# Two-chunk MLP: up-projection as seven half-size products, ScalarE's own GELU, second weight parts on VectorE

## The chip, the cores and the metric

The kernel runs on one core of a Trainium2 chip. The metric is the device time of one execution in microseconds (us): the median over the runs of a kernel. The engines are TensorE (PE, with its weight loads as PEld), VectorE (DVE), ScalarE (ACT), GpSimd (POOL) and SyncE (SP), which issues the DMA transfers. Each engine works through its own queue of instructions in order; a wait on another engine holds up all that stands behind it in the same queue.

## The reference

The reference is one layer of an encoder (width 1024), applied with the same weights to a sequence of 512 rows and to one of 1024. The layer has a mixer (windowed attention and gated linear attention, one input projection, one output projection) and then a gated MLP. The change lies in the MLP:

```python
h = rmsnorm(x, n_ffn_pre)
a, g = jnp.split(h @ w_up, 2, axis=-1)          # w_up: 1024 x 5632
a = dwconv_centred(a, conv_w, conv_b)           # width 3 along the rows of the sequence
f = (jax.nn.gelu(a, approximate=True) * g) @ w_down   # w_down: 2816 x 1024
return x + rmsnorm(f, n_ffn_post)
```

## The kernel before

**Chunks and stages.** Rows are worked in three chunks of 512: chunk 0 is the first sequence, chunks 1 and 2 are the second. The stages are: the input projection of chunk 0; that of chunks 1 and 2, woven with the mixer of the first sequence; the output projection of chunk 0; the MLP of chunk 0 (`m0`), woven with the mixer of the second sequence; the output projections of chunks 1 and 2; and last the MLP of chunks 1 and 2 together (L1240), which runs from about 1340 us to the end.

**Three matmuls for one.** Operands are kept as a first part (`hi`, rounded to 16 bits, or to fp32r) and a second part (`lo`, what is left). `mm3` (L348) forms hi x hi, hi x lo and lo x hi. Each matmul takes 128 rows of the inner dimension, 128 output columns (or rows) and 512 rows of a chunk.

**An MLP block.** The 2816 columns of the MLP are 22 blocks of 128. `Mlp.up(b)` (L1029) computes, for both chunks, the block's columns of `a` and then those of `g`: `gemm_fm` (L483) runs over the eight row tiles of `w_up` in two weight units of four tiles, and uses each unit for both chunks, 24 matmuls. So a block has four units and 96 matmuls. The results stay in PSUM and go through these steps, the same for each chunk: ScalarE copies `a` with the middle tap's weight and the bias (L1047); VectorE adds the outer two taps from PSUM and, at the seam of the chunks, one column (L1045); GELU is written out as a square on ScalarE (L1059), a product on VectorE (L1060), tanh on ScalarE (L1064) and a product on VectorE (L1065); VectorE multiplies with `g` from PSUM (L1079); ScalarE rounds to the first part of `f` (L1080), VectorE forms the second (L1083).

**The order.** `ORDER` (L298) runs blocks 0, 1, 2, 3, then the down-projection of group 0 (blocks 0 to 2), then 4, 5, 6, the down-projection of group 1, and so on; the last group has four blocks. A down-projection (`down`, L1095) has a unit for each block and half of the 1024 output columns, each used for the eight row tiles of the two chunks, 24 matmuls; its sums are added to `y` on VectorE (L1115). In the last one `Post` normalises the rows, adds the residual and stores them.

**The weights.** `_Weights` (L70) serves the units in a list written out beforehand (`units_ffn`, L322). At each `next()` it first runs what was set down for later (`later(n, fn)` runs `fn` at the n-th `next()` from then: the steps above hang on this), then forms the first part of the unit three ahead on ScalarE (`_hi`, L107), and the second part of the unit two ahead on VectorE (`_lo`, L113), and issues loads further ahead. A load (`_load`, L86) brings two units, 512 KB, into one of six `w_raw` tiles. First parts have four buffers, second parts three: the first part three units ahead goes into the buffer that the unit before the present one leaves. In the MLP of chunk 0 the weights are also measured, for the scale that takes them into 16 bits (`Group`, L237; `Rows` does the same for the activations).

**Memory around the change.** The tiles that the last stage takes on the right side of the SBUF (`f2`, `two`, L1239) lie where earlier stages had theirs. `load_mix` (L949) loads the mixer's result in eight tiles for each output projection. `attention` has small tiles `m` (8 buffers) and `den` (4).

## Time and profile before

| | |
|---|---|
| median of 3 runs | 2058.14 us (2057.96 to 2066.22) |
| the profiled execution | 2062.58 us |
| its span, first to last instruction | 2060.8 us |
| TensorE busy / granted clock, mean | 1897.4 us (92%) / 0.97 |
| VectorE, ScalarE, GpSimd busy | 1177.3, 968.7, 241.5 us |
| MLP of chunks 1 and 2 | from about 1340 us to the end |

How to read the profile's lines: a group has line, engine, operation, output <- inputs with their shapes, and a count; then busy time in us and the mean of one in ns; then the engine's idle time just before these instructions and what ended it. A line of the timeline has start, duration, engine, line, operation, and in brackets the idle time before it. L351, L352 and L353 are the three matmuls of `mm3`. The names of the activations of chunks 1 and 2 in the last stage are `d` and `c`; `w_hi` and `w_lo` are the parts of the weights, `bank` is a PSUM bank, `ya` the MLP's tile between the steps, `f` its result.

### The profile page before, as it was taken

How to read it: one execution, taken by the hardware profiler on the slowest of the kernel's cores; microseconds unless marked ns; L12 is line 12 of the kernel's file. 1: busy time of each engine (PE TensorE's matmuls, PEld its weight loads, DVE VectorE, ACT ScalarE, POOL GpSimd, SP SyncE). 2: the span in 40 equal slices, each digit the busy share in tenths (PEclk: the TensorE clock that was granted, in tenths of full speed). 3: DMA queues.
4: the chain of work that ended last, by engine and by line, in shares of the span. 5: the costliest groups of instructions: out<-in, count | busy, mean ns of one | idle time of the engine just before them, and what ended most of it. 6: DMA issues, size and time to landing. Idle time of an engine off the chain costs nothing. (4 is left out here: it accounts for less than half of the span.)

```text
span 2060.8 us, 31557 instructions
## 1 busy us (share of the span) xinstructions
PE 1897.4 (92%) x11912; PEld 1184.9 (57%) x11912; DVE 1177.3 (57%) x2363; ACT 968.7 (47%) x1858; POOL 241.5 (12%) x529
## 2 busy tenths in 40 slices
PE   4999899999988787988998999999999999999996
PEld 3486444887754544455565567745565646464655
DVE  4555673342548787886666545764355454545556
ACT  5665564232557776878345335534323232413232
POOL 3112110000222212120110202210000000000002
PEclk9999999999999999999998999999999999999998
DMA  6766984335559999974334268631121111111132
GB/s 199 223 180 164 208 182 138 114 94 196 195 156 167 206 203 183 186 172 143 99 97 135 88 212 285 223 111 44 52 62 41 52 52 52 41 57 57 52 132 83
DMA packets 389613, 274.74 MB, mean 133 GB/s; under 512 B 173874, under 2 KB 342066, under 8 KB 389460
## 3 DMA queue, kind: packets, MB, share of 16 engines
q1 hardware_dynamic: 389460, 272.72, 50.2%
q8 instruction: 94, 1.54, 0.3%
q14 instruction: 59, 0.48, 0.1%
HBM read 191.83 MB, written 47.28 MB: 116 GB/s over the span
## 5 line engine op out<-in xcount | busy, mean ns | idle before, releaser
L351 PE MATMUL bank<-c,w_hi 128*128 128x512 f16 (+1 forms) x816 | 312.4, 383 | 4.4 <-DVE y L1115 3.7
L353 PE MATMUL bank<-c,w_lo 128*128 128x512 f16 (+1 forms) x816 | 311.4, 382 | 4.4 <-DVE w_lo L120 4.4
L352 PE MATMUL bank<-c,w_hi 128*128 128x512 f16 (+1 forms) x816 | 311.4, 382 | 0.0
L353 PEld LDWEIGHTS <-w_lo 128*128 128x128 f16 x1360 | 135.0, 99 | 167.4 <-issue 9.1
L351 PEld LDWEIGHTS <-w_hi 128*128 128x128 f16 x1360 | 135.8, 100 | 158.8 <-issue 11.6
L111 ACT ACTIVATE w_hi<-w_raw,up_up 128x512 f16<-128x512 f32 x176 | 125.8, 719 | 214.5 <-PE bank L352 107.6
L352 PEld LDWEIGHTS <-w_hi 128*128 128x128 f16 x1360 | 135.0, 99 | 158.4 <-issue 14.1
L352 PE MATMUL bank<-w_lo,f 128*128 128x512 f32 x528 | 212.9, 403 | 5.0 <-DVE w_lo L118 5.0
L351 PE MATMUL bank<-w_hi,f 128*128 128x512 f32 x528 | 213.2, 411 | 2.8 <-DVE y L1115 1.8
L353 PE MATMUL bank<-w_hi,f 128*128 128x512 f32 x528 | 211.2, 400 | 0.0
L111 ACT ACTIVATE w_hi<-w_raw 128x512 fp32r<-128x512 f32 x144 | 90.3, 630 | 243.4 <-PE bank L353 191.3
L120 DVE SCALAR_TENSOR_TENSOR w_lo<-w_raw,up_up,w_hi 128x512 f16<-128x512 f32 x176 | 131.3, 748 | 107.4 <-PE bank L353 49.9
L118 DVE TENSOR_TENSOR w_lo<-w_raw,w_hi 128x512 fp32r<-128x512 f32 x144 | 98.5, 687 | 122.0 <-PE bank L352 96.4
L1045 DVE SCALAR_TENSOR_TENSOR ya<-bank,cvt,ya 128x511 f32<-128x511 f32 x176 | 108.0, 614 | 73.8 <-ACT ya L1047 67.5
L1115 DVE TENSOR_TENSOR y<-bank,y 128x512 f32<-128x512 f32 x144 | 96.3, 687 | 88.6 <-PE bank L353 88.4
L353 PE MATMUL bank<-d,w_lo 128*128 128x512 f16 x352 | 133.4, 379 | 0.9 <-DVE w_lo L120 0.9
L351 PE MATMUL bank<-d,w_hi 128*128 128x512 f16 x352 | 133.5, 379 | 0.1
L352 PE MATMUL bank<-d,w_hi 128*128 128x512 f16 x352 | 133.4, 379 | 0.0
L254 ACT ACTIVATE w_junk<-w_raw 128x512 bf16<-128x512 f32 (+1 forms) x136 | 85.3, 627 | 98.5 <-DMA w_raw<-in_w_up_dram 50.0
L352 PEld LDWEIGHTS bank<-w_lo,f 128*128 128x128 f32 x528 | 100.9, 191 | 30.1 <-DVE w_lo L118 8.8
L632 DVE SCALAR_TENSOR_TENSOR p<-t,rs,p 128x512 f16<-128x512 f32 (+2 forms) x96 | 88.5, 925 | 51.2 <-ACT p L625 50.7
L351 PEld LDWEIGHTS bank<-w_hi,f 128*128 128x128 f32 x528 | 100.6, 191 | 29.1 <-ACT y L1113 1.7
(193 smaller groups left out, 3658.8 us busy)
## 6 DMA issues: line engine op xcount, KB each, us to landing
w_raw<-in_w_up_dram SPq DMA_DIRECT2D x88, 512.0 KB, 4.4
w_raw<-in_w_in_dram SPq DMA_DIRECT2D x44, 512.0 KB, 4.4
w_raw<-in_w_down_dram SPq DMA_DIRECT2D x36, 512.0 KB, 4.0
mix<-mx SPq DMA_DIRECT2D x24, 512.0 KB, 9.3
xin<-in_x_sample_dram SPq DMA_DIRECT2D x16, 512.0 KB
w_raw<-in_w_out_dram SPq DMA_DIRECT2D x32, 256.0 KB, 6.2
xin<-x SPq DMA_DIRECT2D x16, 512.0 KB, 4.6
bias<-in_nbias_dram SPq DMA_DIRECT2D x8, 832.0 KB
```

Source lines behind the costliest of these rows:

```text
L111: self.nc.scalar.activation(out=self.hi[i], in_=raw, func=ACTF.Copy, scale=1.0 if group is None else group.scale)
L118: self.nc.vector.tensor_tensor(out=lo, in0=raw, in1=hi.bitcast(F32), op=ALU.subtract)
L120: self.nc.vector.scalar_tensor_tensor(out=lo, in0=raw, scalar=group.scale, in1=hi, op0=ALU.mult, op1=ALU.subtract)
L254: nc.scalar.activation(out=junk[:, :raw.shape[1]], in_=raw, func=ACTF.Square, accum_out=self.sums[:, self.at:self.at + 1])
L351: nc.tensor.matmul(out, ah, bh, start=start, stop=False)
L352: nc.tensor.matmul(out, ah, bl, start=False, stop=False)
L353: nc.tensor.matmul(out, al, bh, start=False, stop=stop)
L632: nc.vector.scalar_tensor_tensor(out=p[:, n:2 * n], in0=t[:, kf:T], scalar=rs, in1=p[:, 0:n], op0=ALU.mult, op1=ALU.subtract)
L1045: nc.vector.scalar_tensor_tensor(out=out, in0=src, scalar=cw[:, j:j + 1], in1=out, op0=ALU.mult, op1=ALU.add)
L1115: nc.vector.tensor_tensor(out=y[t][:, cols], in0=ps[t], in1=y[t][:, cols], op=ALU.add)
```

## The change

In the MLP of chunks 1 and 2, blocks 3 to 21 (`PLAIN = 3`) no longer compute four products of weight halves and activations but seven (the Strassen-Winograd form of a 2 x 2 block product). The weights of a block are four quarters: `a11`, `a12` (upper and lower 512 rows of the columns for `a`), `a21`, `a22` (those for `g`); the activations are four: `b11`, `b21` (chunk 1), `b12`, `b22` (chunk 2). A product is 4 row tiles x 3 matmuls.

- **Weight sums.** A block has seven units. `_prep`, four units ahead, scales the two loaded tiles in place on ScalarE (two copies of 1024 columns) and forms four sums of 512 columns on GpSimd. First parts of all seven are formed on ScalarE as before, second parts of all seven on VectorE, without a scale.
- **Activation sums.** `sums` forms three new quarters `t1` to `t3` (in `quarters`), twelve steps woven with the first blocks, and puts the fourth in the place of `b12` after block 2, four steps issued at once. A step is a GpSimd sum, two VectorE sums, a ScalarE copy and a GpSimd difference.
- **Output sums.** `up7` copies two products out of PSUM on ScalarE, adds the other five on VectorE, each to what is in SBUF, and has two sums on GpSimd. Convolution and product then read from SBUF and not from PSUM.
- **GELU.** With two chunks (blocks 0 to 2 too), square, product, tanh and product become one ScalarE function, `Gelu_apprx_tanh`, and the product with `g` uses the scale without the factor 0.5. The MLP of chunk 0 keeps the old steps.
- **Everywhere.** Second parts are formed three units ahead (`LO` 3, before 2) with four buffers (before 3). Scales leave room for the sums (factor 4). `m` has 6 buffers, `den` 3. The first sequence's output projection holds seven of its eight `mix` tiles at a time (`held`). Gain rows and row tiles are placed in a pool `pre` that is given back before the last stage, which takes `f2`, `two`, `work` and `quarters`. In the last stage `f`'s two steps come at the third and fourth `next()` after a changed block's last product; before, at the second and third.

The core of the diff:

```diff
-    LOAD, SCALE, HI, LO = 1, 2, 3, 2
+    LOAD, SCALE, PREP, HI, LO = 1, 2, 4, 3, 3
...
+    def _prep(self, i):
+        if len(self.units[i]) == 7 or self.units[i][7]:
+            return
+        group, n = self.units[i][5], NK * 64
+        for t in self.block[i]:
+            self.nc.scalar.activation(out=t, in_=t, func=ACTF.Copy, scale=group.scale)
+        a11, a12, a21, a22 = (t[:, k * n:(k + 1) * n] for t in self.block.pop(i) for k in range(2))
...
+            self.nc.gpsimd.tensor_tensor(out=t, in0=x, in1=y, op=op)
...
+        s1 = total(a21, a22, ALU.add)
+        s2 = total(s1, a11, ALU.subtract)
+        s4 = total(a12, s2, ALU.subtract)
+        s3 = total(a11, a21, ALU.subtract)
+        for j, x in enumerate((a11, s1, s2, a12, s4, s3, a22)):
+            self.raw[i + j] = x
...
+        if len(self.units[i]) > 7:
+            self.nc.vector.tensor_tensor(out=lo, in0=raw, in1=hi, op=ALU.subtract)
...
+        self._upto("prep", self._prep, i + self.PREP)
         self._upto("hi", self._hi, i + self.HI)
         self._upto("lo", self._lo, i + self.LO)
...
+            if kind == "up" and n == 2 and i >= PLAIN:
+                for j in range(7):
+                    units.append((w_up, 0, 4, (i * 128, FF + i * 128), 128, G_UP[i], False, j))
...
+        def sums(self, b):
...
+            self.right = (b11, t1, t2, b21, b22, t3, b12)
+            todo = [(t1, b12, b11, ALU.subtract), (t3, b22, b12, ALU.subtract), (t2, t3, b11, ALU.add)]
+            for out, x, y, op in ([(b12, b21, t2, ALU.subtract)] if b else todo):
+                for k in range(n):
+                    hi, lo = (self.work.tile([128, CH], F32, name=nm, tag=nm) for nm in ("u", "v"))
+                    nc.gpsimd.tensor_tensor(out=hi, in0=x[0][:, k], in1=y[0][:, k], op=op)
+                    nc.vector.tensor_tensor(out=lo, in0=x[1][:, k], in1=y[1][:, k], op=op)
+                    nc.vector.tensor_tensor(out=hi, in0=hi, in1=lo, op=ALU.add)
+                    nc.scalar.activation(out=out[0][:, k], in_=hi, func=ACTF.Copy)
+                    nc.gpsimd.tensor_tensor(out=out[1][:, k], in0=hi, in1=out[0][:, k], op=ALU.subtract)
+                    yield 1
...
+            def product(j, pool, fn):
+                wh, wl = W.next()
+                xh, xl = self.right[j]
+                ps = bank(pool)
+                for k in range(NK // 2):
+                    mm3(ps, (wh[:, k, :], wl[:, k, :]), (xh[:, k], xl[:, k]), k == 0, k == NK // 2 - 1)
+                later(1, lambda: fn(ps))
...
+            def p6(ps):
+                add(u, ps, x)
+                nc.gpsimd.tensor_tensor(out=y, in0=u, in1=v, op=ALU.add)
+
+            def p7(ps):
+                add(u, ps, u)
+                nc.gpsimd.tensor_tensor(out=v, in0=u, in1=v, op=ALU.add)
+            product(0, dense, lambda ps: keep(x, ps))
+            yield 1
+            product(1, dense, lambda ps: keep(v, ps))
+            yield 1
+            product(2, spare_banks, p6)
+            yield 1
+            product(3, dense, lambda ps: add(x, ps, x))
+            yield 1
+            product(4, dense, lambda ps: add(y, ps, y))
+            self.act(b, two, [x, y], (2, 3))
+            yield 1
+            product(5, spare_banks, p7)
+            yield 1
+            product(6, spare_banks, lambda ps: add(u, ps, u))
+            self.gate(b, two, f, [u, v], (3, 4))
+            yield 1
...
+            def whole(i):
+                nc.scalar.activation(out=two[i][:, 1], in_=two[i][:, 0], func=ACTF.Gelu_apprx_tanh)
+            for at, fn in zip(steps, (conv, poly, gelu) if n == 1 else (conv, whole)):
...
+                else:
+                    yield from self.up(i)
+                    _run(self.sums(i))
...
-            box["mix"] = list(load_mix(0, box["mx"], 8))
+            box["mix"] = held(load_mix(0, box["mx"], 7), 7)
...
+    _weave(m12.run(ORDER), m12.sums(0), 20, 12)
```

More of the change, by code (lines that the diff above doesn't have):

```diff
@@ L87, in _load @@
         if i in self.raw:
+            return
+        if len(self.units[i]) > 7:
+            if self.units[i][7] == 0:
+                self.block[i] = [self._whole(i, c0) for c0 in self.units[i][3]]
             return
@@ L108, in _hi @@
         raw, group = self.raw[i], self.units[i][5]
+        whole = len(self.units[i]) > 7
         hi = self.pool.tile([128, self.width], F32R if group is None else FP16, name="w_hi", tag="w_hi", bufs=4)
         self.hi[i] = hi[:, :raw.shape[1]]
[L111 removed]
+        self.nc.scalar.activation(out=self.hi[i], in_=raw, func=ACTF.Copy,
+                                  scale=1.0 if group is None or whole else group.scale)
     def _lo(self, i):
         raw, hi, group = self.raw[i], self.hi.pop(i), self.units[i][5]
[L115 removed]
+        lo = self.pool.tile([128, self.width], F32R if group is None else FP16, name="w_lo", tag="w_lo", bufs=4)
         lo = lo[:, :raw.shape[1]]
[L117 removed]
+        if len(self.units[i]) > 7:
+            self.nc.vector.tensor_tensor(out=lo, in0=raw, in1=hi, op=ALU.subtract)
+        elif group is None:
             self.nc.vector.tensor_tensor(out=lo, in0=raw, in1=hi.bitcast(F32), op=ALU.subtract)
@@ L954, in load_mix, with held, rest @@
             yield t
+    def held(tiles, n):
+        ready = [next(tiles) for _ in range(n)]
+        def rest():
+            yield ready.pop(0)
+            while ready:
+                ready.extend(t for t in [next(tiles, None)] if t is not None)
+                yield ready.pop(0)
+        return rest()
     class Post:
@@ new lines, in up7, with add, keep @@
+        def up7(self, b):
+            f = [f(b) for _, _, f, _ in self.chunks]
+            self.f[b] = f
+            two = [pool.tile([128, 2, CH], F32, name="ya", tag="two") for pool in self.two]
+            u, v = (self.work.tile([128, CH], F32, name=nm, tag=nm) for nm in ("u", "v"))
+            x, y = (t[:, 1] for t in two)
+            def product(j, pool, fn):
[5 more added lines that the diff above has]
+                later(1, lambda: fn(ps))
+            def add(out, ps, x):
+                nc.vector.tensor_tensor(out=out, in0=ps, in1=x, op=ALU.add)
+            def keep(out, ps):
+                nc.scalar.activation(out=out, in_=ps, func=ACTF.Copy)
+            def p6(ps):
[20 more added lines that the diff above has]
+            yield 1
@@ L1039, in up, with act @@
             yield from gemm_fm([(c[1], pa) for c, pa in zip(self.chunks, pas)])
+            self.act(b, two, pas, (1, 2, 3))
+            yield n
+            pgs = [bank(self.banks[i]) for i in range(n)]
+            yield from gemm_fm([(c[1], pg) for c, pg in zip(self.chunks, pgs)])
+            self.gate(b, two, f, pgs, (2, 3))
+            yield n
+        def act(self, b, two, pas, steps):
+            cw, n = cvt[:, b, :], len(self.chunks)
             def conv(i):
@@ L1065, in gelu, with gate @@
                 nc.vector.scalar_tensor_tensor(out=s, in0=s, scalar=1.0, in1=ya, op0=ALU.add, op1=ALU.mult)
-            def each(steps, fn):
+            def whole(i):
+                nc.scalar.activation(out=two[i][:, 1], in_=two[i][:, 0], func=ACTF.Gelu_apprx_tanh)
+            for at, fn in zip(steps, (conv, poly, gelu) if n == 1 else (conv, whole)):
                 for i in range(n):
-                    later(steps, lambda i=i: fn(i))
-            each(1, conv)
-            each(2, poly)
-            each(3, gelu)
-            yield n
-            pgs = [bank(self.banks[i]) for i in range(n)]
-            yield from gemm_fm([(c[1], pg) for c, pg in zip(self.chunks, pgs)])
+                    later(at, lambda i=i, fn=fn: fn(i))
+        def gate(self, b, two, f, pgs, steps):
+            undo = G_UP[b].undo[:, 1:2] if len(self.chunks) == 1 else G_UP[b].undo[:, 0:1]
             def prod(i):
                 s, fh = two[i][:, 1], f[i][0]
-                nc.vector.scalar_tensor_tensor(out=s, in0=s, scalar=G_UP[b].undo[:, 1:2], in1=pgs[i], op0=ALU.mult, op1=ALU.mult)
+                nc.vector.scalar_tensor_tensor(out=s, in0=s, scalar=undo, in1=pgs[i], op0=ALU.mult, op1=ALU.mult)
                 nc.scalar.activation(out=fh, in_=s, func=ACTF.Copy)
@@ L1083, in rest @@
                 nc.vector.tensor_tensor(out=f[i][1], in0=two[i][:, 1], in1=f[i][0].bitcast(F32), op=ALU.subtract)
-            each(2, prod)
-            each(3, rest)
-            yield n
+            for at, fn in zip(steps, (prod, rest)):
+                for i in range(len(self.chunks)):
+                    later(at, lambda i=i, fn=fn: fn(i))
         def residual(self, i):
@@ L1136, in run @@
             for kind, i in order:
-                yield from (self.up(i) if kind == "up" else self.down(i))
+                if kind == "down":
+                    yield from self.down(i)
+                elif len(self.chunks) == 1 or i >= PLAIN:
+                    yield from (self.up if len(self.chunks) == 1 else self.up7)(i)
+                elif i < PLAIN - 1:
+                    yield from self.up(i)
+                else:
+                    yield from self.up(i)
+                    _run(self.sums(i))
     def after(n, gen):
```

63 lines of the change are left out of this document (41 added, 22 removed).

## The prediction

> **What bounds the kernel now.** I read the page's busy shares and slices first, then a table of busy time by stage, then the groups of instructions and the timeline inside the last stage, where the change lies.
>
> ```profile
> PE 1897.4 (92%) x11912; PEld 1184.9 (57%) x11912; DVE 1177.3 (57%) x2363; ACT 968.7 (47%) x1858; POOL 241.5 (12%) x529
> ```
>
> ```profile
> PE   4999899999988787988998999999999999999996
> ```
>
> ```profile
> 1331.00:1995.00 664.00, 659.95 (x2999) 371.77 (x2998) 348.24 (x539) 213.67 (x337) 7.11 (x14) 1.00 0.19 57
> 610.00:930.00 320.00, 273.60 (x1400) 154.17 (x1400) 258.85 (x620) 241.12 (x452) 71.80 (x182) 0.95 0.96 183
> ```
>
> The columns of the last fence are stretch, length, busy PE, PEld, DVE, ACT, POOL, granted clock, DMA share, GB/s. From 1331 to 1995 us, nearly the whole two-chunk MLP, TensorE has work for 659.95 of 664 us at a clock of 1.00, while VectorE is busy 348, ScalarE 214 and GpSimd 7 us. There the time is the number of matmuls times their spacing. Busy time per matmul overstates the spacing, since neighbours overlap, so I take it from starts:
>
> ```profile
> 1500.02 0.38 PE L351 MATMUL bank<-d,w_hi 128*128 128x512 f16 x1
> ...
> 1519.87 0.38 PE L353 MATMUL bank<-c,w_lo 128*128 128x512 f16 x1
> ...
> 1520.32 0.39 PE L352 MATMUL bank<-w_lo,f 128*128 128x512 f32 x1
> ...
> 1552.94 0.39 PE L352 MATMUL bank<-w_lo,f 128*128 128x512 f32 x1
> ```
>
> The first pair is 92 spacings apart: 19.85 / 92 = 0.2158 us for an up-projection matmul. The second is 141 apart: 32.62 / 141 = 0.2313 us for a down-projection one.
>
> ```profile
> L352 PE MATMUL bank<-d,w_hi 128*128 128x512 f16 x337 | 127.7, 379 | 0.0
> L352 PEld LDWEIGHTS <-w_hi 128*128 128x128 f16 x673 | 65.9, 98 | 78.6
> ```
>
> L352 has 673 weight loads here for the matmuls of both chunks (337 of `d` and 336 of `c`): each matmul already loads its own 128 columns. A product that serves one activation matrix therefore loses no shared load, and 0.2158 us holds for the new products.
>
> **TensorE: the gain.** An up block is 2 column blocks x 2 chunks x 8 row tiles x 3 = 96 matmuls; as seven products it is 7 x 4 x 3 = 84. Nineteen of 22 blocks change: 19 x 12 = 228 matmuls x 0.2158 = **49.2 us** less, if everything else stays hidden. A changed block has 18.1 us instead of 20.7, and one product 12 x 0.2158 = 2.59 us.
>
> **VectorE and ScalarE in a changed block.** Rows from 1360 to 1995 us (the wide ACT row and the table load from the whole run):
>
> ```profile
> L1045 DVE SCALAR_TENSOR_TENSOR ya<-bank,cvt,ya 128x511 f32<-128x511 f32 x84 | 62.9, 748 | 62.7 <-ACT ya L1047 62.0
> L120 DVE SCALAR_TENSOR_TENSOR w_lo<-w_raw,up_up,w_hi 128x512 f16<-128x512 f32 x82 | 61.2, 748 | 80.7 <-PE bank L353 41.8 <-issue 23.5 <-PE bank L352 14.5
> L1115 DVE TENSOR_TENSOR y<-bank,y 128x512 f32<-128x512 f32 x80 | 55.3, 691 | 84.2 <-PE bank L353 84.0
> L1079 DVE SCALAR_TENSOR_TENSOR ya<-ya,undo_up,bank 128x512 f32<-128x512 f32 x42 | 31.3, 744 | 17.4 <-PE bank L353 17.4
> L1065 DVE SCALAR_TENSOR_TENSOR ya<-ya 128x512 f32<-128x512 f32 x44 | 30.4, 692 | 2.4
> L1060 DVE SCALAR_TENSOR_TENSOR ya<-ya 128x512 f32<-128x512 f32 x43 | 29.5, 687 | 16.0 <-ACT ya L1059 16.0
> L1083 DVE TENSOR_TENSOR f<-ya,f 128x512 fp32r<-128x512 f32 x42 | 29.1, 692 | 28.5 <-ACT f L1080 28.5
> L118 DVE TENSOR_TENSOR w_lo<-w_raw,w_hi 128x512 fp32r<-128x512 f32 x38 | 26.1, 688 | 15.6 <-PE bank L352 12.3 <-PE bank L353 2.9
> L1045 DVE SCALAR_TENSOR_TENSOR ya<-bank,cvt,ya 128x1 f32<-128x1 f32 x42 | 9.1, 216 | 5.1 <-PE bank L353 5.1
> ```
>
> ```profile
> L111 ACT ACTIVATE w_hi<-w_raw,up_up 128x512 f16<-128x512 f32 x81 | 57.8, 722 | 159.9 <-PE bank L352 76.8 <-DVE y L1115 72.9 <-DVE ya L1045 9.6
> L1047 ACT ACTIVATE ya<-bank,cvt 128x512 f32<-128x512 f32 x42 | 32.3, 769 | 44.4 <-PE bank L353 44.4
> L1059 ACT ACTIVATE ya<-ya 128x512 f32<-128x512 f32 x43 | 26.8, 623 | 20.8 <-DVE ya L1045 20.8
> L1080 ACT ACTIVATE f<-ya 128x512 fp32r<-128x512 f32 x42 | 26.4, 630 | 67.5 <-DVE ya L1079 67.5
> L111 ACT ACTIVATE w_hi<-w_raw 128x512 fp32r<-128x512 f32 x39 | 24.6, 632 | 105.6 <-PE bank L353 66.1 <-PE bank L352 39.0
> L1113 ACT ACTIVATE y<-bank 128x512 f32<-128x512 f32 x16 | 9.6, 598 | 18.8 <-PE bank L353 18.2
> ```
>
> ```profile
> L376 ACT ACTIVATE junk<-xin 128x1024 bf16<-128x1024 f32 x24 | 25.1, 1047 | 12.2 <-DMA xin<-x 12.0
> ```
>
> ```profile
> 955.31 1.28 ACT L1064 ACT_TABLE_LOAD   x1
> ```
>
> VectorE, before: 4 second parts x 0.748, 4 taps x 0.748, 2 edges x 0.216, polynomial 2 x 0.687, GELU end 2 x 0.692, product 2 x 0.744, `rest` 2 x 0.692 = 12.0 us of 20.7. After: 7 second parts x 0.688 (4.8), 5 sums out of PSUM x 0.691 (3.5), taps and edges as before (3.4), product and `rest` (2.9): **14.6 us of 18.1**. ScalarE, before: 4 x 0.722 + 2 x (0.769 + 0.623 + 0.623 + 0.630) = 8.2. After: 2 scaled copies of 1024 columns at 1.047 plus 0.09 for the scale operand (0.722 - 0.632), 7 first parts x 0.632, 2 copies out of PSUM x 0.598, 2 x (0.769 + 0.623 + 0.630): **11.9 us of 18.1**. Both fit, and the down blocks between give slack. The built-in GELU was not run; I take the 0.623 us of the ScalarE functions in its place. Its table costs one load, 1.28 us in the last row; were tables loaded twice a block, ScalarE would have 14.5 of 18.1 us, still hidden.
>
> **GpSimd, and the price of sharing with VectorE.** GpSimd now adds 128x512 tiles: four for the weights and two for the outputs of each block.
>
> ```profile
> 562.04 4.25 POOL L476 TENSOR_TENSOR stg<-stg,gg 128x512 f32<-128x512 f32 x3 [3.31 <-DVE stg L475]
> 583.41 0.73 POOL L476 TENSOR_TENSOR stg<-stg,gg 128x256 f32<-128x256 f32 x1
> L476 POOL TENSOR_TENSOR stg<-stg,gg 128x512 f32<-128x512 f32 x6 | 9.0, 1516 | 16.6 <-DVE stg L475 16.6
> ```
>
> ```profile
> 562.48 0.74 DVE L361 SCALAR_TENSOR_TENSOR c<-bank,rows_fpre,c 128x512 f16<-128x512 f32 x1
> 564.39 0.78 DVE L120 SCALAR_TENSOR_TENSOR w_lo<-w_raw,up_tm,w_hi 128x544 f16<-128x544 f32 x1
> 583.57 1.15 DVE L120 SCALAR_TENSOR_TENSOR w_lo<-w_raw,up_tm,w_hi 128x544 f16<-128x544 f32 x1
> 587.01 0.79 DVE L120 SCALAR_TENSOR_TENSOR w_lo<-w_raw,up_tm,w_hi 128x544 f16<-128x544 f32 x1 [1.49 <-PE bank L352]
> ```
>
> With GpSimd idle the `w_lo` step, which has both inputs in SBUF, takes 0.79 us; started 0.16 us after a GpSimd sum it takes 1.15, ending about 0.6 us after that sum. In the other order VectorE keeps its 0.78 us, and the three GpSimd sums around it take 4.25 us: 1.16 to 1.42 each, without and with it. The L361 step, which reads one input from PSUM, keeps its 0.74 us during those sums. I price a sum at 1.24 us (at most the 1.52 of the group's mean), 7.4 us a block, during which a VectorE instruction with both inputs in SBUF stands still: the seven second parts, `rest`, and now the taps and the product too, whose inputs move from PSUM to SBUF; the five sums out of PSUM go on. The Trainium skill has this as a rule (SBUF — State Buffer, Who interferes with whom): a VectorE instruction with two SBUF inputs and a GpSimd one that reads SBUF take a shared port in turn, and the later one is blocked until the other ends. By that rule, the trace agrees; it speaks against this change.
>
> By hand, in queue order: weight parts are formed three products ahead, a cover of 7.8 us. The four weight sums of the next block start at product 3 and take 5.0 us; less the 1.4 us of the two PSUM sums that run beside them and some idle time, they hold VectorE up by about 3 us until product 6; there convolution, a sum and a second part ask 4.8 us in 2.6, and the last sum waits about 1 us for GpSimd to read `u`. Together that is 14.6 + 3 + 1 = 18.6 us against 18.1. Counted from the start of product 3 in the middle block of three: both `rest` and the first sum end at 1.9 us; the second part at 3.8, behind its first part (two scaled copies and itself, 2.9) and a GpSimd sum; the next sum and second part at 5.6, the next pair at 7.5, each with a GpSimd sum between; taps and edges with one more GpSimd sum from 8.7 to 12.8; the sum at 13.5, GpSimd's `v` at 14.7, the second part at 15.3. TensorE wants that part at the end of two more products, 4 x 2.59 + 2 x 2.59 = 15.5. So I charge **3 us** for the six runs of three, with 0 and 15 as ends; the 15 is one more GpSimd sum (1.24 us) in the way twice in each run.
>
> **The quarter sums.** Twelve steps run beside the first blocks, four (`sums(2)`) are issued at once before block 3. In each, GpSimd, VectorE, ScalarE and GpSimd follow one another: 1.24 + 0.69 + 0.63 + 1.24, and four hand-overs of 0.08:
>
> ```profile
> 2046.32 0.08 issue
> ```
>
> ```profile
> 545.00:550.00 5.00, 0.80 (x5) 0.59 (x4) 2.48 (x3) 1.79 (x3) 0.73 (x2) 0.79 0.98 376
> 550.00:555.00 5.00, 5.00 (x27) 3.90 (x26) 2.43 (x3) 3.56 (x6) 1.28 (x3) 0.53 0.77 245
> ```
>
> That is 4.1 us a step. The twelve have 10 units of 5.18 us and fit. The four hold VectorE's queue, with the second part of block 3's fourth product behind them: 1.4 + 3 x 4.1 + 1.3 = 15 us after VectorE reaches them, which is 1.5 to 4 us into the last unit of block 2 (its own weight parts, 1.4 us, and up to 2.6 us of lag). TensorE has weights for 5.2 + 3 x 2.6 = 13.0 us from there, so it waits 3.5 to 6 us, once. After the 4.2 us gap at 545 us above, the clock of the next 5 us is 0.53, 2.4 us lost. The Trainium skill has this (TensorE: Matmul & The Clock Gate, Part 1): a window of about 3.4 us without work halves the clock until a busy one has passed. The trace agrees. I charge **8 us** (0 to 12).
>
> **What else moves.** Everywhere the second part is now formed one unit earlier (`LO` 3, four buffers), in the same call as its first part, so VectorE waits up to 0.72 us a unit for ScalarE, with the attention steps queued behind it. From 610 to 930 us VectorE has 61 us idle, of which it costs some; more lead helps TensorE. I charge **2 us** (-3 to +10), near the low end since most of that idle time is spent in waits already. Fewer `m` and `den` buffers are in that bound. The eighth `mix` tile of the first sequence loads after the first is free, with weight loads behind it on SyncE's queue; it has 6 x 24 x 0.2313 = 33 us until its use, so nothing (one load's length if that cover went). The weight traffic is the same 1 MB a block. The end, where `f` of the last block comes one unit later, and the start of the quarter sums beside the last `Post` steps: **1 us** (0 to 4).
>
> Sum: -49.2 + 3 + 8 + 2 + 1 = **-35 us**. The profiled execution took 2062.6 us (span 2060.8), 4.4 above the median; I take the difference from the median 2058.1: **2023 us**, its own range 2015 to 2032.
>
> **The rivals.**
> 1. All of it is hidden: for it, that VectorE idled for TensorE in most rows above; 2058.1 - 49.2 = 2009 us, 2007 to 2014. Chance 0.18.
> 2. The shared port sets the pace in the runs of three, and the change ends slower. If all GpSimd time stopped VectorE, at 1.52 us a sum, a block would ask 14.6 + 9.1 = 23.7 us against 18.1: 16.8 behind per run, less 7.8 of cover, 9 us x 6 = 54, and 2.4 us of halved clock after each of perhaps two gaps a run, 29: +83 + 11 - 49 = +45, about 2103 us. It ends slower once a run loses over 6.4 us. Against it: the five sums out of PSUM run meanwhile, and GpSimd's sums come in bunches. Chance 0.06. Half as bad, with 2 to 6 us lost per run, 2032 to 2056: 0.12, half of it above 2048.
> 3. The earlier second parts slow the first two thirds by 10 to 20 us: for it, 61 idle us of VectorE in 320; 2031 to 2041, rarely over 2048. Chance 0.10.
> 4. The change doesn't save matmuls at their spacing, because a product of 12 ends in a wait: no row above shows one at a change of unit; with one hand-over of 0.08 us at each of 19 x 7 = 133 products it would cost 11 us, 2034. Chance 0.02.
>
> **How the numbers follow.** Forecast 0.52; rivals 0.18, 0.06 and 0.12, 0.10, 0.02. A measurement of this kernel tells about 0.5% (10.3 us) from no change. Faster: 0.52 + 0.18 + 0.06 + 0.08 + 0.02 = 0.86; same: 0.06 + 0.02 = 0.08; slower 0.06. The range 2008 to 2046 leaves out the worst of both port cases and a little below, about 0.15.
>
> **What would show it.** Right: 228 fewer f16 matmuls, spacing still 0.216; GpSimd about 7 us busy per block; one gap of some 5 us near block 3, with a low clock after it; VectorE near 15 us busy of 18 in a changed block. Wrong: TensorE waiting for `w_lo` in every run of three; the clock under 0.97 after 1400 us; `w_lo` means well over 0.8 us; the two-chunk MLP starting over 5 us later than its 1340 us before; table loads in every block.

## The result and the profile after

The changed kernel takes 2004.49 us (median of 4 runs, 1992.94 to 2006.38) beside 2058.05 us for the kernel before (4 runs): 53.6 us less by the medians, and a ratio of 0.9723 by the means, 95% interval 0.9676 to 0.9770. The forecast was 35 less, and the result lies 3.5 us below its range. Of all the runs below, one (of the kernel with only a fourth buffer) took 2389.96 us at a granted clock of 0.752, where the others have 0.96 to 0.98; it is left out of that kernel's figures. The profiled execution took 2005.52 us with a span of 2003.7; before it was 2062.58 with 2060.8.

The busy line and TensorE's slices of the page, after:

```profile
PE 1845.8 (92%) x11684; PEld 1160.3 (58%) x11684; DVE 1286.0 (64%) x2459; ACT 1036.3 (52%) x1964; POOL 457.0 (23%) x675
PE   5999899999989888889889999988999999999997
```

11912 - 11684 = 228 matmuls are gone, as counted. GpSimd's busy time has nearly doubled. Where the time went is seen by splitting the span at the first matmul of the two-chunk MLP, the first that reads `d`. The rows of TensorE's instructions on `d` from 1280 to 1360 us, before and then after (the first time of each row is the start):

```profile
L351 PE MATMUL bank<-d,w_hi x17: 377/379/379, 1340.1 to 1359.4; 128*128 128x512 f16 x17
```

```profile
L395 PE MATMUL bank<-d,w_hi x27: 379/379/487, 1316.0 to 1359.9; 128*128 128x512 f16 x27
```

Of the 57.1 us between the spans, **24.1 us are gained before the MLP starts**, in stages whose computation the change leaves alone; the MLP itself goes from 720.7 to 687.7 us, **33.0 less instead of 49.2**. Below, "MLP" is this stretch, from the first matmul on `d` to the end of the span.

The table by stage, after (length, busy PE, PEld, DVE, ACT, POOL, granted clock, DMA share, GB/s):

```profile
1331.00:1995.00 664.00, 645.41 (x2884) 376.39 (x2881) 477.21 (x666) 288.43 (x459) 229.06 (x163) 0.99 0.20 63
1340.00:1460.00 120.00, 103.77 (x445) 56.49 (x444) 81.86 (x95) 54.53 (x87) 59.85 (x41) 0.96 0.15 43
1460.00:1940.00 480.00, 479.76 (x2170) 276.32 (x2169) 342.85 (x487) 207.01 (x318) 153.17 (x101) 1.00 0.18 54
```

The last row holds most of the changed blocks, with runs of three among them: TensorE is busy for 479.76 of 480 us at a clock of 1.00. Most of what the MLP loses lies in the row above it: 16 us without a matmul in 120, at a clock of 0.96. There the last plain blocks, the quarter sums of the activations and the first changed block meet. TensorE's waits in that stretch, after (total, times, longest, in us):

```profile
PE bank L395 <- DVE ya L1177: 7.4, 2, 6.2
PE bank L397 <- DVE w_lo L152: 4.8, 2, 3.9
PE bank L396 <- DVE w_lo L154: 2.3, 1, 2.3
```

VectorE is behind, with taps (L1177) and second parts (L152, L154). The timeline of the first of these gaps, GpSimd and then VectorE:

```profile
1336.01 3.71 POOL L1099 TENSOR_TENSOR quarters<-u,quarters 128x512 f16<-128x512 f32 x2 [4.74 <-ACT quarters L1098]
1339.68 2.27 POOL L1095 TENSOR_TENSOR u<-c,d 128x512 f32<-128x512 f16 x2
1341.90 1.72 POOL L120 TENSOR_TENSOR w_sum<-w_raw 128x512 f32<-128x512 f32 x1
```

```profile
1340.87 1.63 DVE L1097 TENSOR_TENSOR u<-u,v 128x512 f32<-128x512 f32 x1 [2.17 <-POOL u L1095]
1342.42 0.86 DVE L1177 SCALAR_TENSOR_TENSOR ya<-bank,cvt,ya 128x511 f32<-128x511 f32 x2
```

A quarter sum's step (L1097) stands in VectorE's queue ahead of block 0's taps. It waits 2.17 us for GpSimd, then takes 1.63 us for what is 0.69 us of work; the taps that free TensorE's bank come after it. GpSimd runs the steps close together, with block 3's weight sums (L120) already among them.

VectorE's groups from 1460 to 1940 us, after (count, then busy us and mean ns):

```profile
L1177 DVE SCALAR_TENSOR_TENSOR ya<-ya,cvt 128x511 f32<-128x511 f32 x68 | 60.6, 892 | 4.8 <-ACT ya L1179 3.5
L152 DVE TENSOR_TENSOR w_lo<-w_sum,w_hi 128x512 f16<-128x512 f32 x69 | 54.1, 785 | 36.2 <-ACT w_hi L144 36.1
L152 DVE TENSOR_TENSOR w_lo<-w_raw,w_hi 128x512 f16<-128x512 f32 x52 | 44.6, 858 | 0.0
L1121 DVE TENSOR_TENSOR ya<-bank,ya 128x512 f32<-128x512 f32 x34 | 23.3, 684 | 8.7 <-PE bank L397 8.7
L1215 DVE TENSOR_TENSOR f<-ya,f 128x512 fp32r<-128x512 f32 x34 | 22.8, 682 | 0.0
L1211 DVE SCALAR_TENSOR_TENSOR ya<-ya,undo_up,v 128x512 f32<-128x512 f32 x17 | 18.7, 1099 | 19.9 <-ACT w_hi L144 14.0 <-POOL v L1132 5.9
L1177 DVE SCALAR_TENSOR_TENSOR ya<-ya,cvt 128x1 f32<-128x1 f32 x34 | 14.6, 429 | 0.0
L1211 DVE SCALAR_TENSOR_TENSOR ya<-ya,undo_up,u 128x512 f32<-128x512 f32 x17 | 12.7, 745 | 0.2
```

The sums out of PSUM (L1121) keep their 0.684 us beside GpSimd; the taps, whose inputs are now both in SBUF, went from 748 to 892 ns, the product of `v` from 744 to 1099. With these means a changed block asks VectorE for 7 second parts x 0.816 (the mean of the two L152 groups), 4 taps x 0.892, 2 edges x 0.429, 5 sums x 0.684, a product of each kind and 2 `rest` x 0.682 (L1215): 16.8 us of 18.1, which is 2.2 us over the forecast's 14.6. It fits. Such a sum counts every step at its whole length, while neighbours overlap by some 0.08 us: in the timeline above the taps start 1.55 us after a step that lasts 1.63. By that, the 22 steps of a block keep VectorE for about 15 us (an estimate).

### The profile page after: what moved, and what is told of

Read it like the earlier page. It is cut to its first block, busy times and chain, and to the rows that moved or that the text cites. A ratio compares the mean times of both kernels' runs of the same rounds, so it can differ in the third digit from the quotient of the medians.

```text
span 2003.7 us, 31673 instructions
## 1 busy us (share of the span) xinstructions
PE 1845.8 (92%) x11684; PEld 1160.3 (58%) x11684; DVE 1286.0 (64%) x2459; ACT 1036.3 (52%) x1964; POOL 457.0 (23%) x675
## 5 line engine op out<-in xcount | busy, mean ns | idle before, releaser
L395 PE MATMUL bank<-c,w_hi 128*128 128x512 f16 (+1 forms) x664 | 255.3, 385 | 15.4 <-DVE y L1247 8.4
L396 PE MATMUL bank<-c,w_hi 128*128 128x512 f16 (+1 forms) x664 | 255.0, 384 | 0.0
L397 PE MATMUL bank<-c,w_lo 128*128 128x512 f16 (+1 forms) x664 | 254.2, 383 | 0.0
L144 ACT ACTIVATE w_hi<-w_raw 128x512 fp32r<-128x512 f32 (+1 forms) x201 | 125.6, 627 | 194.0 <-PE bank L397 136.4
L395 PEld LDWEIGHTS <-w_hi 128*128 128x128 f16 x1284 | 129.1, 101 | 162.9 <-issue 18.2
L396 PEld LDWEIGHTS <-w_hi 128*128 128x128 f16 x1284 | 128.0, 100 | 154.7 <-issue 21.1
L154 DVE TENSOR_TENSOR w_lo<-w_raw,w_hi 128x512 fp32r<-128x512 f32 x144 | 104.9, 734 | 108.7 <-ACT w_hi L144 106.6
L395 PEld LDWEIGHTS bank<-w_hi,f 128*128 128x128 f32 x528 | 100.7, 191 | 29.9 <-DVE y L1247 2.4
L397 PEld LDWEIGHTS bank<-w_hi,f 128*128 128x128 f32 x528 | 100.7, 191 | 22.6
L669 ACT ACTIVATE p<-t,rs 128x512 f16<-128x512 f32 (+2 forms) x96 | 81.6, 857 | 60.7 <-DMA pt<-p 50.7
L120 POOL TENSOR_TENSOR w_sum<-w_raw 128x512 f32<-128x512 f32 x38 | 55.2, 1452 | 221.7 <-DVE w_lo L152 197.5
L144 ACT ACTIVATE w_hi<-w_raw,up_up 128x512 f16<-128x512 f32 x100 | 71.4, 715 | 61.6 <-PE bank L396 34.2
L156 DVE SCALAR_TENSOR_TENSOR w_lo<-w_raw,up_up,w_hi 128x512 f16<-128x512 f32 x100 | 78.3, 786 | 30.4 <-ACT w_hi L144 27.9
L152 DVE TENSOR_TENSOR w_lo<-w_sum,w_hi 128x512 f16<-128x512 f32 x76 | 60.2, 792 | 55.7 <-ACT w_hi L144 55.5
```

What stands on the lines that cost most here:

```text
L120: self.nc.gpsimd.tensor_tensor(out=t, in0=x, in1=y, op=op)
L144: self.nc.scalar.activation(out=self.hi[i], in_=raw, func=ACTF.Copy, scale=1.0 if group is None or whole else group.scale)
L152: self.nc.vector.tensor_tensor(out=lo, in0=raw, in1=hi, op=ALU.subtract)
L154: self.nc.vector.tensor_tensor(out=lo, in0=raw, in1=hi.bitcast(F32), op=ALU.subtract)
L156: self.nc.vector.scalar_tensor_tensor(out=lo, in0=raw, scalar=group.scale, in1=hi, op0=ALU.mult, op1=ALU.subtract)
L395: nc.tensor.matmul(out, ah, bh, start=start, stop=False)
```

## The experiments

For the early gain the theory was that the weights' second part, formed a unit earlier, brings it; the rivals, that it is chance, or the fourth buffer that goes with it. For the MLP's loss there were three candidates: the quarter sums stand in a bad place and lack room, which I held first; the weight sums beside the first changed blocks; or the quarter sums are dear in themselves, because VectorE's steps with two SBUF inputs stand still beside GpSimd. Totals scatter, because the stretch before the MLP does: in nine profiles, of the changed kernel and of its variants whose edits lie in the MLP, the MLP starts anywhere from 1304.2 to 1320.5 us. So beside the ratio to the kernel before, measured on the same chip, stands the length of the MLP.

### The second part a unit earlier, alone

```diff
-    LOAD, SCALE, HI, LO = 1, 2, 3, 2
+    LOAD, SCALE, HI, LO = 1, 2, 3, 3
-        lo = self.pool.tile([128, self.width], ..., name="w_lo", tag="w_lo", bufs=3)
+        lo = self.pool.tile([128, self.width], ..., name="w_lo", tag="w_lo", bufs=4)
```

> The kernel before with one edit: second parts of the weights formed three units ahead with four buffers, as in the changed kernel; nothing else of the change. In the two profiles the two-chunk MLP starts 24 us earlier after the change (1340.1 against 1316.0 us). Theory: that is the work of this edit, so this kernel is 18 to 28 us faster than before (about 2034 us), its two-chunk MLP starts near 1318 us and takes the same 720 us from there. Rival: the 24 us are scatter between executions or come from the other small edits (seven mix tiles, the pool that is given back, fewer m and den buffers): then this kernel stays within 5 us of 2058. My prediction had +2 us here (-3 to +10 slower).

Measured: 2032.91 us beside 2054.46, ratio 0.9896 (0.9869 to 0.9923): **21.5 us less** with no other edit, as the theory had it. The MLP starts at 1312.5 us, and is 713.1 us long, 7.6 less than before, which the theory did not have. TensorE's waits for `w_lo` before 1340 us, first in the kernel before, then in this one:

```profile
PE bank L352 <- DVE w_lo L118: 4.5, 5, 2.0
PE bank L353 <- DVE w_lo L120: 4.4, 4, 2.7
PE bank L352 <- DVE w_lo L120: 1.6, 2, 1.2
```

```profile
PE bank L352 <- DVE w_lo L118: 2.0, 1, 2.0
```

10.5 us of them become 2.0, and all of TensorE's waits there fall from 144 to 131.6 us. The mean granted clock of the two profiled executions rises from 0.970 to 0.977, which on 2060 us would be worth up to some 14; over all runs of the two kernels it is 0.971 and 0.974, some 6. How the gain divides between waits and clock is not shown, and 8.5 us fewer waits for `w_lo` are not all of it.

### The fourth buffer, alone

```diff
-        lo = self.pool.tile([128, self.width], ..., name="w_lo", tag="w_lo", bufs=3)
+        lo = self.pool.tile([128, self.width], ..., name="w_lo", tag="w_lo", bufs=4)
```

> The kernel before with a fourth buffer for the second parts and nothing else (they are still formed two units ahead, LO 2). Theory (the 21.5 us of the run with both edits come from forming the second part a unit earlier): ratio 0.998 to 1.002, the first matmul of d in the two-chunk MLP at about 1340 us as before. Rival (the fourth buffer alone lets VectorE form the part before TensorE has released the third): ratio 0.989 to 0.992, the MLP at about 1313 us.

Measured: 2041.84 us beside 2054.62, ratio 0.9943 (0.9919 to 0.9967), 12.8 us less; the MLP starts at 1319.7 us and is 716.3 long. Neither expectation held: the buffer alone brings about half of the 21.5 us, and forming the part earlier the other half. With three buffers VectorE must wait for a release before it writes the next part, and the rows of before in the prediction have it idle for TensorE's matmuls ahead of these parts (L120). But TensorE's waits before 1340 us do not show the gain: they are 142.4 us in all beside 144, and 10.3 for `w_lo` beside 10.5. The short ones for L120 fall from 6.0 to 0.2 us; those for L118 rise, by one of 6.8 us that may be chance in a single profile:

```profile
PE bank L352 <- DVE w_lo L118: 10.1, 3, 6.8
```

Nor does the granted clock rise, 0.969 in the mean of these runs beside 0.970. By which way the buffer gains its 12 us is not shown.

### The changed kernel with the second part as late as before

```diff
-    LOAD, SCALE, PREP, HI, LO = 1, 2, 4, 3, 3
+    LOAD, SCALE, PREP, HI, LO = 1, 2, 4, 3, 2
-        lo = self.pool.tile([128, self.width], ..., name="w_lo", tag="w_lo", bufs=4)
+        lo = self.pool.tile([128, self.width], ..., name="w_lo", tag="w_lo", bufs=3)
```

> The changed kernel with that one edit undone: second parts two units ahead, three buffers. Theory that the early gain is this edit: 20 to 28 us slower than the changed kernel (about 2028 us), with the two-chunk MLP starting near 1340 us; a few us more if the two units of cover do not hide VectorE in the runs of three. Rival (scatter or the other small edits): within 5 us of 2004, starting near 1316 us.

Measured: 2026.96 us beside 2054.46, ratio 0.9859 (0.9832 to 0.9887), against 0.9723 with the edit: some 25 us are given back, as the theory had it, but 13.0 of them in the MLP (700.7 us long). The MLP starts at 1325.7 us, 9.7 later than in the changed kernel, where the theory had 24. TensorE's waits from 1310 to 1980 us, this kernel:

```profile
PE bank L397 <- DVE w_lo L156: 9.7, 4, 6.3
PE bank L396 <- DVE w_lo L154: 8.9, 8, 2.8
```

The two-chunk part of the change alone, without its earlier second parts, is worth 1.4% where the whole is worth 2.8%.

### ScalarE's own GELU, alone

```diff
-            each(2, poly)
-            each(3, gelu)
+            each(2, whole)
```

(in the two-chunk MLP only, with the factor of one half that belongs to it)

> The kernel before with ScalarE's own GELU in the two-chunk MLP in place of square, product, tanh and product; nothing else. Theory: VectorE and ScalarE wait for TensorE there, so the time stays within 4 us of before, with some 2.7 us less VectorE time in each of 22 blocks and one more table load. Rival: the function is slower than 0.623 us or its table is reloaded in each block, 2.6 us a block: still hidden, but seen in the rows; slower by over 5 us only if ScalarE's wait reaches TensorE.

Measured: 2055.76 us beside 2054.46, ratio 1.0005 (0.9988 to 1.0023). It takes work from VectorE where VectorE was busy for 348 of 664 us.

### The changed kernel without quarter sums

```diff
-                for k in range(n):
+                for k in range(0):
...
+    for i in range(3):
+        for s in range(2):
+            nc.gpsimd.memset(m12.quarters[:, i, s], 0.0)
```

> The changed kernel with the sixteen steps that form the quarter sums of the activations left out (the three quarters are filled once with zeros, the fourth is left as it is): the products then multiply other numbers, and the time is that of the kernel without those steps. Theory (nearly all of the 16 us that the two-chunk MLP loses against 49.2 us come from these steps, the twelve beside the first blocks and the four before block 3): the MLP takes 672 to 676 us instead of 687.7, total 1988 to 1994. Rival (the weight sums on GpSimd and VectorE's steps beside them cost it at the first changed blocks): the MLP still takes 682 us or more.

This kernel leaves the sixteen steps out and fills the three quarters with zeros once, so its products multiply other numbers. Measured: 1987.47 us beside 2054.62, ratio 0.9678 (0.9652 to 0.9704). The stretch that lost 16 us, in this kernel:

```profile
1340.00:1460.00 120.00, 120.00 (x548) 66.23 (x547) 60.69 (x87) 56.02 (x87) 27.17 (x18) 1.00 0.16 48
```

TensorE has no gap, though the first changed blocks and their weight sums are there. The MLP is 665.8 us, **21.9 less** than with the sums, and shorter than the theory had it. By whole times the size is less sure: the two medians, taken on different chips, differ by 17.0 us, the two ratios by 0.0045, some 9 us, with intervals that overlap. But the gaps are gone: so the weight sums are not to blame; the sixteen steps are. Now the account of the MLP closes: 720.7 - 49.2 (matmuls) - 7.6 (the first experiment) + 21.9 (quarter sums) = 685.8, and 687.7 were measured.

### The last four steps woven into block 3

```diff
-                else:
-                    yield from self.up(i)
-                    _run(self.sums(i))
...
+                elif i == PLAIN:
+                    yield from _along(self.up7(i), self.sums(i))
```

> The changed kernel with the last four activation sums no longer issued at once before block 3 but one after each of its first four products; the product that needs them is the seventh. In the changed kernel the two-chunk MLP takes 688 us where 49 us less than before would be 671; TensorE is full from 1460 us on, so the 16 us are lost before. Theory: the burst of four steps in front of block 3's weight parts loses 6 to 10 of them; this kernel is 4 to 10 us faster than the changed one. Rival: they are lost to the slow steps as such (two-input VectorE steps of 1.6 us beside GpSimd), wherever they stand: within 2 us of the changed kernel.

Measured: 1999.79 us beside 2054.46, ratio 0.9730 (0.9703 to 0.9757): by the ratio the same as the changed kernel, though the median is 4.7 us lower. The MLP is 684.1 us, 3.6 less; the gap before block 0's taps, 6.2 us, is still there. That the four steps are issued at once, to which the forecast gave its 8 us, is a small part.

### The twelve steps later

As the one above, and

```diff
-    _weave(m12.run(ORDER), m12.sums(0), 20, 12)
+    _weave(m12.run(ORDER), after(3, m12.sums(0)), 24, 15)
```

> The changed kernel with the twelve quarter-sum steps started about 12 us later and spread to the end of the three plain blocks, and the last four put one after each of block 3's first products. Theory (the first gap comes from the sum steps that stand in VectorE's queue beside the last steps of the one-chunk MLP and wait for GpSimd): the gap before the first taps goes, the MLP takes 676 to 680 us, total 1992 to 1998. Rival (the chain of a step, GpSimd and VectorE in turn, asks 65 us of 62 wherever it starts, so what is saved at the start is lost at block 3): 684 us or more, total 2000 or more.

Measured: 1997.73 us beside 2054.62, ratio 0.9734 (0.9710 to 0.9758), MLP 684.1 us, the rival's length, though the total falls into the theory's range. The first gap went, and others came. TensorE's longest waits from 1340 to 1460 us, this kernel:

```profile
PE bank L395 <- ACT quarters L1098: 6.9, 1, 6.9
PE bank L396 <- DVE w_lo L154: 2.1, 1, 2.1
PE bank L397 <- DVE w_lo L152: 1.6, 2, 1.2
```

Now block 3's products wait for the quarters themselves.

### One more plain block for them

```diff
-    PLAIN = 3
+    PLAIN = 4
...
+                if kind == "down" and i == 0 and len(self.chunks) == 2:
+                    yield from _along(self.down(i), self.sums(1))
...
+    _weave(m12.run(ORDER), after(3, m12.sums(0)), 30, 15)
```

> The changed kernel with one more plain block (four instead of three): the twelve steps are spread over the four, and the last four steps stand beside the down-projection that comes between block 3 and block 4. One block more at full size costs 12 x 0.2158 = 2.6 us. Theory (the sums lose their 16 us only for want of room): the MLP takes 675 to 679 us, total 1991 to 1996. Rival (the steps cost VectorE and GpSimd the same wherever they stand): 687 us or more, total 2004 or more.

Measured: 1999.63 us beside 2054.62, ratio 0.9746 (0.9720 to 0.9772), MLP 686.3 us, nearer to the rival. The room of a fourth block, 20 us, bought nothing: my theory of want of room fell here. Its plain blocks are shown two experiments further down.

### The same sums without GpSimd, three plain blocks

In the kernel with the later steps:

```diff
-                    nc.gpsimd.tensor_tensor(out=hi, in0=x[0][:, k], in1=y[0][:, k], op=op)
+                    nc.vector.tensor_tensor(out=hi, in0=x[0][:, k], in1=y[0][:, k], op=op)
...
-                    nc.gpsimd.tensor_tensor(out=out[1][:, k], in0=hi, in1=out[0][:, k], op=ALU.subtract)
+                    if prev:
+                        p, q = prev
+                        nc.vector.tensor_tensor(out=out[1][:, q], in0=p, in1=out[0][:, q], op=ALU.subtract)
+                    prev = hi, k
...
```

> As the run with the later and woven quarter-sum steps, but GpSimd's two instructions of each of the sixteen steps are given to VectorE, the second of them put behind the next step's sums. VectorE then has 4 instructions of about 0.69 us a step, 2.8 us; with 9.3 us a plain block for the rest that is 28 + 12 x 2.8 = 62 us in the 62 us of three plain blocks. Theory (the steps are dear because VectorE's steps with two SBUF inputs stand still beside GpSimd, so the same sums without GpSimd cost less): the MLP takes 670 to 678 us, total 1986 to 1993. Rival (VectorE's own work is what the blocks have no room for): 684 us or more, total 2000 or more.

Measured: 1991.39 us beside 2056.75, ratio 0.9684 (0.9657 to 0.9711), MLP 678.8 us: 5.3 us of MLP less than with GpSimd's help, though VectorE has twice as many of these instructions. It falls just above the theory's range. VectorE is busy without a break from 1340 to 1380 us, and block 3 still waits for the fourth quarter. The window and the longest wait, this kernel:

```profile
1340.00:1380.00 40.00, 39.11 (x182) 17.57 (x181) 40.00 (x67) 18.17 (x30) 0.99 (x1) 1.00 0.06 20
```

```profile
PE bank L396 <- DVE c L1105: 4.1, 1, 4.1
```

### The same sums without GpSimd, four plain blocks

The edits of the last two experiments together.

> As the run with four plain blocks and the last four steps beside the first down-projection, with all quarter sums on VectorE alone: 37 + 12 x 2.8 = 71 us of VectorE in 83, and four steps in a stretch in which it has little else. Theory (sharing with GpSimd is the price): TensorE has no gap over 2 us between block 0 and block 4, the MLP takes 668 to 672 us (its 663.9 without any loss, and 2.6 for the block at full size), total 1984 to 1989. Rival (the steps cost the same wherever and by whomever): 684 us or more, total 2000 or more.

Measured: **1983.62 us beside 2056.75, ratio 0.9638 (0.9607 to 0.9668)**: the fastest of all, with an interval below the changed kernel's. The MLP is 666.7 us, a little under the theory's range, where 720.7 - 49.2 - 7.6 + 2.6 = 666.5 was to be had without any loss. This run and the one with four plain blocks and GpSimd are the clean pair. First that one, 1320 to 1380 us, the window and the groups of the sums:

```profile
1320.00:1380.00 60.00, 53.96 (x248) 23.77 (x246) 59.38 (x70) 23.55 (x36) 35.71 (x26) 1.00 0.18 58
```

```profile
L1097 DVE TENSOR_TENSOR u<-u,v 128x512 f32<-128x512 f32 x14 | 15.7, 1126 | 0.4 <-POOL u L1095 0.4
L156 DVE SCALAR_TENSOR_TENSOR w_lo<-w_raw,up_up,w_hi 128x512 f16<-128x512 f32 x11 | 9.8, 896 | 0.0
L1096 DVE TENSOR_TENSOR v<-c 128x512 f32<-128x512 f16 x4 | 6.5, 1641 | 0.0
L1215 DVE TENSOR_TENSOR f<-ya,f 128x512 fp32r<-128x512 f32 x4 | 3.7, 920 | 0.0
```

Then the kernel with all sums on VectorE:

```profile
1320.00:1380.00 60.00, 60.00 (x280) 27.20 (x278) 59.91 (x102) 29.97 (x45) 1.10 (x1) 1.00 0.22 68
```

```profile
L156 DVE SCALAR_TENSOR_TENSOR w_lo<-w_raw,up_up,w_hi 128x512 f16<-128x512 f32 x13 | 9.6, 745 | 0.1
L1098 DVE TENSOR_TENSOR u<-u,v 128x512 f32<-128x512 f32 x14 | 9.6, 683 | 0.0
L1221 DVE TENSOR_TENSOR f<-ya,f 128x512 fp32r<-128x512 f32 x6 | 3.9, 685 | 0.0
L1097 DVE TENSOR_TENSOR v<-c 128x512 f32<-128x512 f16 x4 | 2.7, 684 | 0.0
```

VectorE's busy share is the same, 59.4 and 59.9 of 60 us, but it finishes 70 instructions in the one and 102 in the other. The same sum of two SBUF tiles takes 1641 ns beside GpSimd and 684 without it. In the four rows of the first kernel 14 x 0.443 + 11 x 0.151 + 4 x 0.957 + 4 x 0.235 = 12.6 us of "busy" are standing still, which no idle column shows. TensorE is without a matmul for 6.0 of the 60 us there, and for none in the other. The Trainium skill's rule (SBUF — State Buffer, Who interferes with whom), that the later of the two is blocked until the other ends, agrees with this pair (1641 beside 684 ns).

Standing still is not the whole of it. In the kernel with GpSimd's help TensorE's longest wait of the MLP comes later, beside the down-projection with the last four steps (the wait, then two lines of VectorE's timeline):

```profile
PE bank L395 <- DVE ya L1211: 7.8, 1, 7.8
```

```profile
1404.12 1.62 DVE L1097 TENSOR_TENSOR u<-u,v 128x512 f32<-128x512 f32 x1 [3.75 <-POOL u L1095]
1406.79 1.62 DVE L1097 TENSOR_TENSOR u<-u,v 128x512 f32<-128x512 f32 x1 [1.04 <-POOL u L1095]
```

Here VectorE is idle, 3.75 and then 1.04 us, because a step needs GpSimd's sum, and the product that frees TensorE's bank (L1211) stands behind these steps in its queue. So GpSimd's share costs in two ways, by stretched steps and by waits from engine to engine. Both go when VectorE does the sums alone; how much each is worth the runs do not tell.

### Twice as many of GpSimd's weight sums

```diff
-            self.nc.gpsimd.tensor_tensor(out=t, in0=x, in1=y, op=op)
+            for _ in range(2):
+                self.nc.gpsimd.tensor_tensor(out=t, in0=x, in1=y, op=op)
```

> The changed kernel with each of the four weight sums of a changed block issued twice, so that GpSimd has 10 instead of 6 sums a block (same result, written twice). Theory (the runs of three have room: VectorE's steps are only stretched, second parts from 748 to 785 ns and taps from 748 to 892, and the sums out of PSUM go on meanwhile): 0 to 8 us more than the changed kernel, total 2003 to 2012. Rival (as forecast, every GpSimd sum holds up VectorE's steps with two SBUF inputs for its own length): VectorE's 18.6 us become over 23 of 18.1, 9 us lost in each of six runs of three and more for the clock, total 2055 or more.

Measured: 2035.12 us beside 2056.75, ratio 0.9895 (0.9865 to 0.9925), MLP 720.5 us: 32.8 us more than the changed kernel, between the two expectations. The window and TensorE's waits from 1460 to 1940 us, and VectorE's groups that changed most there (lines are one higher in this kernel):

```profile
1460.00:1940.00 480.00, 459.74 (x2041) 264.18 (x2040) 355.17 (x454) 187.75 (x291) 238.90 (x157) 0.99 0.17 51
```

```profile
PE bank L397 <- DVE w_lo L155: 13.7, 10, 2.3
PE bank L396 <- ACT w_hi L145: 5.7, 5, 1.4
```

```profile
L1178 DVE SCALAR_TENSOR_TENSOR ya<-ya,cvt 128x511 f32<-128x511 f32 x64 | 82.4, 1287 | 3.7 <-ACT ya L1180 2.2
L153 DVE TENSOR_TENSOR w_lo<-w_sum,w_hi 128x512 f16<-128x512 f32 x62 | 52.8, 852 | 33.6 <-ACT w_hi L145 33.6
L153 DVE TENSOR_TENSOR w_lo<-w_raw,w_hi 128x512 f16<-128x512 f32 x47 | 48.6, 1034 | 0.0
L1212 DVE SCALAR_TENSOR_TENSOR ya<-ya,undo_up,v 128x512 f32<-128x512 f32 x15 | 16.2, 1079 | 42.5 <-POOL v L1133 30.9 <-ACT w_hi L145 11.7
```

With these means (taps 1.287, second parts 0.930 on average, the rest as in the changed kernel) the steps of a block add up to 19.1 us of 18.1, against 16.8 in the changed kernel; less the overlap of neighbours that is about 17.4, still under 18.1. The last row has what comes on top: VectorE waits 30.9 us in 15 blocks for GpSimd's `v`, where it waited 5.9 in 17. So VectorE falls behind, and TensorE waits some 20 us in 480, 2.3 at most at a time. Whether the longer steps or the longer waits tip it is not separated; that GpSimd's added sums do, is shown.

### The weight sums on VectorE

```diff
-            self.nc.gpsimd.tensor_tensor(out=t, in0=x, in1=y, op=op)
+            self.nc.vector.tensor_tensor(out=t, in0=x, in1=y, op=op)
```

> The changed kernel with the four weight sums of a changed block on VectorE instead of GpSimd: 14.6 + 4 x 0.69 = 17.4 us of VectorE in 18.1, and GpSimd's two output sums left. Theory (GpSimd's weight sums cost VectorE less than doing them itself, but both fit): within 5 us of the changed kernel, 2000 to 2010. Rival (without the four sums on the shared port VectorE's steps go back to 0.69 to 0.75 us and the first changed blocks get shorter): 1990 to 1997. If VectorE at 17.4 of 18.1 us can't keep the order that TensorE needs, 2015 or more, with waits for w_lo in each run of three.

Measured: 1997.39 us beside 2056.75, ratio 0.9715 (0.9688 to 0.9742), MLP 682.7 us: between the two expectations, by the ratio the changed kernel's time within what can be told, and TensorE full from 1460 to 1940 us. In this kernel:

```profile
1460.00:1940.00 480.00, 480.00 (x2172) 280.28 (x2171) 350.97 (x552) 208.45 (x320) 58.41 (x34) 1.00 0.21 65
```

```profile
L1177 DVE SCALAR_TENSOR_TENSOR ya<-ya,cvt 128x511 f32<-128x511 f32 x68 | 50.8, 748 | 5.4 <-ACT ya L1179 4.5
```

VectorE does 65 instructions more than in the changed kernel in 8.1 us more, since the taps are back at 748 ns: 0.12 us for each. Giving the four sums to GpSimd saves VectorE almost nothing here.

## Why the prediction was wrong

**TensorE's gain: right.** 228 matmuls, at 0.2158 us, 49.2 us; TensorE full from 1460 to 1940 us, and the best kernel's MLP within 0.2 us of the length that this count gives.

**The second part formed a unit earlier: the step that failed.** The forecast said "I charge 2 us (-3 to +10)". The runs show -21.5 us by itself, about half of it from the fourth buffer. The step looked at what VectorE would lose by waiting for ScalarE, and wrote "more lead helps TensorE" without pricing it, though TensorE's waits for `w_lo` before the MLP, 10.5 us of them, stood in the trace of before. They would have given the sign, and not the size: they are half of what came. This one term, 23.5 us off, is more than the whole miss of 18.6; the other terms together came out 5 us dearer than charged, and hid some of it. The third rival, which had the same edit slow the first two thirds by 10 to 20 us, had the sign wrong.

**The quarter sums: mis-sized, and in the wrong place.** 8 us were charged for the four steps before block 3, 1 for the start and the end, and nothing for the twelve: "The twelve have 10 units of 5.18 us and fit." The sixteen cost 21.9 us of MLP in the profiles (9 to 17 by whole times), and the largest gap, 6.2 us before block 0's taps, comes where of the sixteen only the twelve run; how the cost divides between the twelve and the four is not separated. The step gave GpSimd's sum 1.24 us and VectorE's 0.69, and took the blocks' own VectorE work as it stood. But beside GpSimd's sums VectorE's steps with two SBUF inputs take up to 1.64 us, the blocks' own second parts and `rest` 0.90 and 0.92 in the mean (the kernel with four plain blocks), and VectorE waits for GpSimd with the blocks' work behind it in its queue. The forecast had the shared port, and applied it to the runs of three alone.

**The runs of three: 3 us charged, none found.** The direction was right (taps 748 to 892 ns), and the doubled sums show that there is an edge: four weight sums a block cost TensorE nothing, eight cost it 20 us in 480. The forecast put 18.6 us into a block: 14.6, 3 of standing still and 1 of waiting for GpSimd. The rows have 2.2 for the second and 0.35 for the third (5.9 us in 17 blocks, for `v` at L1132), and the 14.6 counts 22 steps at their whole lengths, some 1.8 us too much by the overlap of neighbours. A GpSimd sum itself takes longer than the 1.24 us taken: 33 of the weight sums have a mean of 1425 ns, and with the others (1.48 to 1.74 us) GpSimd is busy for about 9 us a block, not 7.

**What was to show it.** One gap of 5 us near block 3 was expected; there were several, from block 0 on. The MLP starts 24 us earlier, and not later. A clock under 0.97 after 1400 us was named as a sign against the forecast, and it is there, 0.91 from 1400 to 1420 us, behind those gaps. One load of ScalarE's table and 0.62 us for the GELU came as taken:

```profile
1344.11 1.28 ACT L1200 ACT_TABLE_LOAD   x1
```

```profile
L1200 ACT ACTIVATE ya<-ya 128x512 f32<-128x512 f32 x34 | 19.6, 622 | 47.3 <-DVE ya L1177 47.3
```

The sum is then -49.2 + 0 - 21.5 + 17.1 = -53.6, where 17.1 is only what is left over for the quarter sums and the end; it lies between the 9 and the 21.9 us that the run without them gave.

**Left open.** By which way the fourth buffer gains its part of the 21.5 us, how the rest divides between waits removed and clock regained, how GpSimd's cost divides between stretched steps and waits, and why the stretch before the MLP varies by up to 16 us between profiles of the same instructions.

## What to carry to other kernels

Price an edit of a shared helper in every stage that calls it, on both sides: what the engine that works earlier loses, and what the engine that waited for it gains; here that side effect was worth 21.5 us beside the 49.2 of the main one. Before giving elementwise work to GpSimd as a free helper, ask what VectorE does meanwhile: where its inputs are both in SBUF, the helper can cost as much as it saves, and the same sixteen steps on VectorE alone made the MLP 19.6 us shorter. Read an engine's busy share together with its number of instructions: 59.4 us busy with 70 of them and 59.9 with 102 are not the same load.

## What the runs showed of the hardware

A VectorE sum of two 128x512 SBUF tiles takes 684 ns alone and up to 1640 ns beside a chain of GpSimd sums, while one with an input in PSUM keeps 684. The taps' edges of one column went from 216 ns with a PSUM input to 429 with SBUF inputs beside GpSimd, and 364 in the kernel that has only two GpSimd sums a block.
